# A state-space stage in fixed order on VectorE and GpSimd: states in fixed places, powers moved to VectorE, and two changed hand-overs of PSUM banks

## The chip, the cores and the metric

The kernel runs on one core of a Trainium2 chip. The core has a matrix engine (TensorE, PE in the profile), three engines for elementwise work (VectorE or DVE, ScalarE or ACT, GpSimd or POOL), and SyncE (SP), which here only issues loads. Each engine works through its own queue in order. The engines share an on-chip memory (SBUF) and wait for each other by semaphores; matrix products land in PSUM, which the kernel uses as eight banks of 128 x 512 float32. GpSimd does not touch PSUM in this kernel. The metric is the device time of one launch in microseconds, and smaller is better.

## The reference

One decoder layer on a sequence of 1024 tokens of width 1024, then a final RMS norm. From the normed and modulated input, one wide projection makes the inputs of two branches. Branch A gates in blocks of 128 tokens. Branch B is a causal convolution, then a chunked state-space scan:

```python
    decay = segsum_exp(adt)
    cb = jnp.einsum('bclgn,bcsgn->bcgls', cc, bc)
    y_diag = jnp.einsum('bcgls,bcgrls,bcsgrp->bclgrp', cb, decay, xd)
    chunk_states = jnp.einsum('bcsgn,bcgrs,bcsgrp->bcgrpn', bc, decay_to_end, xd)
    chunk_decay = jnp.exp(a_cs[..., -1])
    def step(state, inp):
        cs, cd = inp
        return state * cd[..., None, None] + cs, state
    _, prev_states = lax.scan(step, init, (chunk_states, chunk_decay))
    y_off = jnp.einsum('bclgn,bcgrpn,bcgrl->bclgrp', cc, prev_states, jnp.exp(a_cs))
    ...
    y_b = y_b + xh * d_skip[:, None]
    yz = (y_b * jax.nn.silu(ssm_z)).reshape(b, s, SSM_GROUPS, -1)
    y_b = rms_norm(yz, ssm_norm_w.reshape(SSM_GROUPS, -1))
    merged = jax.nn.sigmoid(g_a) * (y_a @ w_proj_a) + jax.nn.sigmoid(g_b) * (y_b @ w_proj_b)
    return x + gate[:, None, :] * (merged @ w_out)
```

There are 8 groups of 4 heads of 64 channels, 8 chunks of 128 tokens, and a state of 128 per channel. Everything is float32.

## The kernel before, in words

The kernel goes through stages that TensorE sets the pace of: the modulation and norm, a first block product (`v_block`), the other parts of the wide projection, the state-space stage together with branch A's output projection, branch B's output projection, the output product and the final norm. A float32 product is computed as three products of rounded parts (high x high, low x high, high x low; hence the `h` and `l` at the ends of names). The large block products are done in seven products per 2 x 2 blocks, named p1, p5, p6, p3, p7, p2, p4, each over some units k of 128 rows, into four PSUM banks j.

`v_block` (L815, its unit loop at L905 to L936) runs right after `sg`, the evacuations by ScalarE (L473) that free four PSUM banks which it then takes as `vx0` to `vx3`. Its first two units each go over the three terms and within each over the four banks; later units go bank by bank.

The state-space stage (class `Group`, L1040) works in 32 steps: groups in pairs, the two groups of a pair in turn, four steps of two chunks each. One step consists of:

- `fetch` (L1046): SP loads the five inputs `sl` and the decay exponents `dcy` into one of five buffers (`NSET = 5`), so a load waits until the step that used the buffer has read it for the last time, in the product yz on GpSimd (L1157).
- `decay` (L1062): ScalarE makes `ea` (L1067), GpSimd cuts off the upper triangle of `dcy` (the mask, an affine_select, L1070), ScalarE exponentiates (L1075).
- `prep` (L1077): TensorE makes `pc` and transposes into `pc` and `px` in PSUM. VectorE multiplies `px` into `xd` and `xe` (L1091) and `dcy` by `pc` (L1095); ScalarE copies the second half of `pc` to `bn` (L1097).
- `front` (L1100): TensorE computes `yi` (within a chunk) from `dcy` and `xd`, and `sp` (what a chunk adds to the state) from `xe` and `bn`. For each of the two chunks, GpSimd multiplies the state by the chunk's decay (L1123) and VectorE adds `sp` (L1125; the first state of a group is a copy, L1121). The state after the first chunk is called the middle state here, the one after the second the end state. New states go round through a ring of places `st_r`.
- `back` (L1129): TensorE computes `yn` from the state ahead of each chunk. `evacuate` (L1142): VectorE forms y1 = x * d_skip + yi (L1151, two instructions) and ym = yn * ea (L1155), GpSimd adds them (L1156) and multiplies by the gate into `yz` (L1157).
- `post` (L1159), every second step of a group: the result is stored to `yb_d`, and two tasks are put off: `squares` (L1174; two activations on ScalarE at L1176 in place, which wait until the store has read the data, and an addition on GpSimd at L1177) and `post2` (L1179; TensorE's sum `pq`, `ssq` on VectorE at L1186, and after a group's last part the power -1/2 of its eight norms on GpSimd at L1190). `later(n, f)` puts `f` off by n tasks; a step of the stage runs three (`front`, `back`, `prep`).

The PSUM banks of the stage are handed out in turn: `bank(name)` waits for the readers of the tile that had the bank eight hand-outs ago. So a TensorE instruction can wait for VectorE not because it needs a value but because it needs a bank: `yi` for the bank of an earlier `sp`, say.

Between the parts of a step TensorE is given instructions of branch A's output projection (`proj_a`, L1359; `draw(n)` takes the next n pieces). It accumulates `pma` over 8 k for each of 8 column blocks dd. At k = 1 `wa_block` (L1276) prepares the next block's weights: ScalarE rounds to `wah` (L1280), VectorE subtracts to get `wal` (L1281), each twice. At a block's end VectorE forms `tha` from `pma` (L1382) and stores it.

What sets the order: instructions wrapped in `pin` keep the order of the program; all others are placed on their engine's queue by a planner that goes by priorities (`tc.high_priority()`; `item` at L1410 gives it to every part of a step) and by its own idea of when operands are ready. In the kernel before, VectorE's and GpSimd's instructions of the state-space stage are of the second kind, and so is `wal`.

Branch B's output projection (`multiply`, L1545, matmul at L1552; unit loop from L1666) takes over the eight PSUM banks as `psx` and `psy` when p1 begins. `banks()` (L1443) hands them out in the order y0, y1, y2, x0 to x3, y3. The last `pma` tiles, the last `yn` and the last `pq` still hold some of them then.

The two hand-overs of banks that the diff touches are this order and the order of the first units of `v_block`.

## Time and profile before

| | us |
|---|---|
| median of 3 runs | 1404.81 (1404.6 to 1406.76) |
| profiled execution | 1402.83 |
| its span from first to last instruction | 1401.1 |
| mean clock granted to TensorE | 0.996 of full |

The profile's page gives the busy time of each engine, the span in 40 slices, the DMA queues, the chain of work that ended last, and the costliest groups. Other views give the busy time by windows, the waits of an engine by what ended them, and a timeline of one engine in order, in which the figure in brackets is the engine's idle time just before an instruction and what released it. The stages by time: `v_block` begins at 70.46 us, the state-space stage spans some 918 to 1145 us, and branch B's output projection (p1) begins at 1158.93 us.

| window, us | PE busy | DVE busy | ACT busy | POOL busy |
|---|---|---|---|---|
| 0 to 60 | 54.97 | 33.56 | 38.67 | 3.15 |
| 60 to 100 | 38.70 | 32.10 | 25.25 | 0.00 |
| 1140 to 1160 | 19.01 | 13.14 | 7.48 | 4.19 |
| 1260 to 1330 | 68.66 | 67.44 | 27.69 | 0.00 |

A window in which PE is busy all the time can't become shorter without less work for PE; where it is not, the timeline tells what it waited for.

### The profile page before, as it was taken

How to read it: one execution, taken by the hardware profiler on the slowest of the kernel's cores; microseconds unless marked ns; L12 is line 12 of the kernel's file. 1: busy time of each engine (PE TensorE's matmuls, PEld its weight loads, DVE VectorE, ACT ScalarE, POOL GpSimd, SP SyncE). 2: the span in 40 equal slices, each digit the busy share in tenths (PEclk: the TensorE clock that was granted, in tenths of full speed). 3: DMA queues.
4: the chain of work that ended last, by engine and by line, in shares of the span. 5: the costliest groups of instructions: out<-in, count | busy, mean ns of one | idle time of the engine just before them, and what ended most of it. 6: DMA issues, size and time to landing. Idle time of an engine off the chain costs nothing.

```text
span 1401.1 us, 20579 instructions
## 1 busy us (share of the span) xinstructions
PE 1369.7 (98%) x6971; PEld 1135.3 (81%) x6971; DVE 1055.3 (75%) x1815; ACT 804.7 (57%) x1496; POOL 217.8 (16%) x208
## 2 busy tenths in 40 slices
PE   8999999999999999999999999999999999999997
PEld 7678888888888888878888888888888788888786
DVE  4776776687777889888888795398777655859976
ACT  5754656666666566455675555677676623223453
POOL 0000000000000011211000110038878750000001
PEclk9999999999999999999999999999999999999999
DMA  8775433333434777777775774598887658878913
GB/s 263 197 237 147 120 121 120 105 123 118 135 105 128 225 219 230 220 238 226 215 220 148 241 214 134 179 354 319 279 267 278 220 185 280 319 254 313 378 44 120
DMA packets 277181, 288.62 MB, mean 206 GB/s; under 512 B 15788, under 2 KB 224084, under 8 KB 277076
## 3 DMA queue, kind: packets, MB, share of 16 engines
q1 hardware_dynamic: 182420, 203.76, 45.6%
q10 hardware_dynamic: 94656, 83.54, 18.1%
q8 instruction: 55, 0.90, 0.3%
q14 instruction: 50, 0.41, 0.1%
HBM read 199.79 MB, written 87.46 MB: 205 GB/s over the span
## 4 chain that ended last, share of the span: by engine, by line
PE 78%; DVE 7%; DMA 7%; ACT 3%; issue 3%; POOL 2%; SPq 1%; ACTq 0%; DVEq 0%; POOLq 0%
PE xuz L536 6%; PE xx L536 6%; PE xcb L536 6%; PE xz L536 5%; PE xg L536 5%; PE pma L81 4%; PE yx L536 3%; PE vx L918 3%; PE x L1552 3%; PE yuz L536 3%; PE yp L1552 3%; PE ycb L536 3%; PE yz L536 3%; PE ox L1745 2%; PE yg L536 2%
## 5 line engine op out<-in xcount | busy, mean ns | idle before, releaser
L759 POOL TENSOR_TENSOR wog<-wog,gb 128x256 f32<-128x256 f32 x16 | 21.5, 1362 | 624.0 <-DMA wog<-in_w_out_dram 602.9
L1075 ACT ACTIVATE dcy<-dcy,nacs 128x128 f32<-128x128 f32 x256 | 78.7, 388 | 17.2 <-POOL dcy L1070 16.1
L1070 POOL TENSOR_SCALAR_AFFINE_SELECT dcy<-dcy 128x1024 f32<-128x1024 f32 x32 | 35.0, 1094 | 135.4 <-DMA yl<-ya_d 88.7
L990 ACT ACTIVATE ac<-ac 128x1024 f32<-128x1024 f32 x32 | 33.9, 1060 | 25.8 <-DVE ac L988 22.6
L1067 ACT ACTIVATE ea<-dcy 64x512 f32<-64x512 f32 x64 | 40.0, 626 | 12.2 <-DMA dcy<-acs_d 11.8
L81 PE MATMUL pma<-yh,wah 128*128 128x512 f32 x128 | 43.8, 423 | 0.0
L81 PE MATMUL pma<-yh,wal 128*128 128x512 f32 x128 | 43.2, 419 | 0.0
L1490 DVE SCALAR_TENSOR_TENSOR yn<-yn,par,rb 128x512 f32<-128x512 f32 x32 | 23.9, 747 | 24.8 <-DMA yn<-yb_d 24.8
L1155 DVE TENSOR_TENSOR ym<-yn,ea 128x512 f32<-128x512 f32 (+1 forms) x32 | 19.9, 622 | 29.9 <-PE yn L81 29.7
L1095 DVE TENSOR_TENSOR dcy<-dcy,pc 128x1024 f32<-128x1024 f32 x32 | 38.9, 1217 | 3.8 <-PE pc L84 2.6
L1157 POOL TENSOR_TENSOR yz<-y,sl 128x512 f32<-128x512 f32 x32 | 41.4, 1294 | 1.1
L81 PE MATMUL pma<-yl,wah 128*128 128x512 f32 x128 | 40.3, 396 | 0.0
L1156 POOL TENSOR_TENSOR y<-y,ym 128x512 f32<-128x512 f32 (+1 forms) x32 | 36.6, 1143 | 14.5 <-DVE ym L1155 14.5
L81 PE MATMUL yi<-dcy,xd 128*64 128x128 f32 x512 | 35.9, 284 | 2.9 <-DVE st L1125 2.9
L81 PEld LDWEIGHTS yn<-sl,st 128*128 128x128 f32 x224 | 30.3, 190 | 8.8 <-issue 2.7
L81 PE MATMUL yn<-sl,st 128*128 128x128 f32 x224 | 31.4, 276 | 5.4 <-DVE st L1125 5.4
L81 PE MATMUL sp<-xe,bn 128*128 128x256 f32 x112 | 33.6, 418 | 2.9 <-DVE ssq L1186 1.7
L988 DVE SCALAR_TENSOR_TENSOR ac<-c2x,cwt,ac 128x1023 f32<-128x1023 f32 (+2 forms) x24 | 31.2, 1298 | 5.7 <-ACT ac L986 5.6
L1760 POOL TENSOR_TENSOR r<-r,fnw 128x512 f32<-128x512 f32 x2 | 2.5, 1296 | 208.2 <-ACT junk L1758 208.2
L988 DVE SCALAR_TENSOR_TENSOR ac<-c2cb,cwt,ac 128x1023 f32<-128x1023 f32 (+2 forms) x24 | 31.1, 1294 | 4.8 <-ACT ac L986 4.7
L1123 POOL TENSOR_TENSOR st<-st,cd 128x256 f32<-128x256 f32 x48 | 32.5, 677 | 11.2 <-PE yn L81 7.1
L952 ACT ACTIVATE vm<-vm,vr 128x128 f32<-128x128 f32 x64 | 25.8, 483 | 14.0 <-DMA vm<-v_d 13.5
...
## 6 DMA issues: line engine op xcount, KB each, us to landing
...
```

The costliest lines, as they stand in the source:

```text
L81: pin(PE.matmul(acc, l, r, start=first, stop=last))
L536: pin(PE.matmul(ps, lw[:, k * P : (k + 1) * P], r[k], start=first and n + k == 0, stop=n == 2 and k == 3, skip_group_check=not first))
L918: pin(PE.matmul(ps[pn][j], l[:, js], r, start=nm in ("p1", "p5", "p2") and n + k == 0, stop=n == 2 and k == 3, skip_group_check=nm not in ...
L988: V.scalar_tensor_tensor(ac[:, s:], cc[:, : S - s], conv_wt[:, 3 - s, i : i + 1], ac[:, s:], op0=ALU.mult, op1=ALU.add)
L990: A.activation(ac, ac, AF.Silu)
L1067: A.activation(ea[hh * HD : (hh + 1) * HD], dcy.rearrange("p (j e) i l -> p e j (i l)", e=2)[hh * HD : (hh + 1) * HD, hh], AF.Exp)
L1070: G.affine_select(out=d8, in_=d8, compare_op=ALU.is_ge, fill=-1e30, base=0, pattern=[[0, 2 * HPG], [1, P]], channel_multiplier=-1)
L1075: A.activation(dcy[:, h, i, :], dcy[:, h, i, :], AF.Exp, bias=sub[:, i, h : h + 1])
L1095: V.tensor_tensor(d3, d3, pc[:, 0:256].unsqueeze(1).to_broadcast([P, HPG, 256]), op=ALU.mult)
L1156: G.tensor_add(y1[:, :, t0:], y1[:, :, t0:], m[:, :, t0:])
L1157: G.tensor_mul(yz, y1, sl[:, 4:6])
L1552: pin(PE.matmul(ps[j], a[:, v, js], r, start=first and n + k == 0, stop=n == 2 and k == KT - 1, skip_group_check=not first))
```

## The change

In `v_block`, the first two units' matmuls are drawn together: first the eight high x high and low x high products of both units on banks 0 and 1, then the rest. In the state-space stage VectorE's and GpSimd's instructions are pinned to the order of the program (those of `prep` not in the first pair's first step). The order in `prep` becomes `dcy` times `pc`, then `bn` (now copied by VectorE), then `xd`, `xe`. States live in six fixed places, three for each group of a pair: one for the middle state and two in turn for the end state. `front` now adds the middle state, issues GpSimd's multiplication for the end state, and forms y1, which was in `evacuate`. A new `close`, called after `back`, adds `sp` to the end state (so behind ym on VectorE) and issues GpSimd's multiplication for the next step's middle state. `squares` is put off by 8 tasks instead of 5. The power -1/2 is made by 11 small VectorE instructions (128 x 8) instead of one on GpSimd: a first guess from the exponent bits, then three rounds of three. The subtraction `wal` is pinned at k = 3 and k = 4 of `proj_a`. At the start of p1, PSUM banks are handed out in the order y0, y2, x0 to x3, y3, y1.

VectorE's instructions become 120 more (32 copies and 8 x 11 small ones), ScalarE's 32 fewer and GpSimd's 8 fewer.

```diff
                 ps["y"] = [bank(f"vy{j}") for j in range(4)]
-            (bh, bl), (wh, wl) = (bop[bn][v][k] for v in range(2)), wops[u]
-            terms = list(enumerate(((bh, wh), (bl, wh), (bh, wl))))
-            for j, (n, (l, r)) in [(j, t) for t in terms for j in range(4)] if u < 2 else [(j, t) for j in range(4) for t in terms]:
-                js = slice(j * P, (j + 1) * P)
-                pin(PE.matmul(ps[pn][j], l[:, js], r, start=nm in ("p1", "p5", "p2") and n + k == 0,
+            at = [(u, n, j) for j in range(4) for n in range(3)]
+            if u == 0:
+                ends = [(0, 2, 0), (0, 2, 1)] + [(0, n, j) for j in (2, 3) for n in range(3)]
+                at = [(i, n, j) for i in range(2) for n in range(2) for j in range(2)] + ends
+            elif u == 1:
+                at = [(1, 2, 0), (1, 2, 1)] + [(1, n, j) for j in (2, 3) for n in range(3)]
+            for i, n, j in at:
+                (bh, bl), (wh, wl) = (bop[bn][v][units[i][1]] for v in range(2)), wops[i]
+                l, r = ((bh, wh), (bl, wh), (bh, wl))[n]
+                pin(PE.matmul(ps[pn][j], l[:, j * P : (j + 1) * P], r, start=nm in ("p1", "p5", "p2") and n + units[i][1] == 0,
                               stop=n == 2 and k == 3, skip_group_check=nm not in ("p1", "p5", "p2")))
-            wops.pop(u)
+            if u:
+                wops.pop(u)
...
     NSET = 5
-    nstep, nst = [0], [0]
+    nstep = [0]
...
                 tp(px[:, i * 256 + P : i * 256 + 256], sl[:, 3, tsl], ident)
+            keep = pin if s or g > 1 else lambda i: i
             x4 = px.rearrange("p (i h w) -> p i h w", i=2, h=HPG)
             xs = []
+            d3 = dcy.rearrange("p h i l -> p h (i l)")
+            keep(V.tensor_tensor(d3, d3, pc[:, 0:256].unsqueeze(1).to_broadcast([P, HPG, 256]), op=ALU.mult))
+            bn = p2x.tile([P, 256], F32, name=f"bn{nm}", tag="bn", bufs=2)
+            keep(V.tensor_copy(bn, pc[:, 256:512]))
             for v, f in (("xd", dthq), ("xe", dde)):
                 t = p2x.tile([P, 512], F32, name=f"{v}{nm}", tag=v, bufs=3)
-                V.tensor_tensor(t.rearrange("p (i h w) -> p i h w", i=2, h=HPG), x4,
-                                fac(f, g, s).unsqueeze(3).to_broadcast([P, 2, HPG, HD]), op=ALU.mult)
+                keep(V.tensor_tensor(t.rearrange("p (i h w) -> p i h w", i=2, h=HPG), x4,
+                                     fac(f, g, s).unsqueeze(3).to_broadcast([P, 2, HPG, HD]), op=ALU.mult))
                 xs.append(t)
-            d3 = dcy.rearrange("p h i l -> p h (i l)")
-            V.tensor_tensor(d3, d3, pc[:, 0:256].unsqueeze(1).to_broadcast([P, HPG, 256]), op=ALU.mult)
-            bn = p2x.tile([P, 256], F32, name=f"bn{nm}", tag="bn", bufs=3)
-            A.copy(bn, pc[:, 256:512])
             self.pre[s] = (sl, dcy, bn, xs[0], xs[1], ea)
...
             sp = bank(f"sp{nm}")
-            self.y[s] = yi
-            self.sts = [self.st]
-            for i in range(2 if s < NCH // 2 - 1 else 1):
+            last = s == NCH // 2 - 1
+            for i in range(1 if last else 2):
                 mm(sp[:, i * 256 : (i + 1) * 256], bn[:, i * P : (i + 1) * P], xe[:, i * 256 : (i + 1) * 256])
-            for i in range(2 if s < NCH // 2 - 1 else 1):
-                pool, tag, b = st_r[nst[0] % 4 if nst[0] % 4 < 3 else 2]
-                nst[0] += 1
-                s2 = pool.tile([P, 512 if pool is hp else 256], F32, name=f"st{nm}_{i}", tag=tag, bufs=b)[:, 0:256]
-                if self.st is None:
-                    V.tensor_copy(s2, sp[:, 0:256])
-                else:
-                    G.tensor_mul(v3(s2), v3(self.st),
-                                 fac(cd, g, s)[:, i].unsqueeze(2).to_broadcast([P, HPG, HD]))
-                    V.tensor_add(s2, s2, sp[:, i * 256 : (i + 1) * 256])
-                self.st = s2
-                self.sts.append(s2)
+            mid, *ends = state(g % 2)
+            if s == 0:
+                pin(V.tensor_copy(mid, sp[:, 0:256]))
+            else:
+                pin(V.tensor_add(mid, mid, sp[:, 0:256]))
+            self.sts = [self.st, mid]
+            self.st = ends[s % 2]
+            if not last:
+                pin(G.tensor_mul(v3(self.st), v3(mid), fac(cd, g, s)[:, 1].unsqueeze(2).to_broadcast([P, HPG, HD])))
+            self.y1 = y1 = turn(y1_r, f"y1{nm}", F32).rearrange("p (j t) -> p j t", j=2)
+            for j in range(2):
+                pin(V.scalar_tensor_tensor(y1[:, j], sl[:, 2 + j], dskt[:, 2 * g + j : 2 * g + j + 1],
+                                           yi[:, j * 256 : (j + 1) * 256], op0=ALU.mult, op1=ALU.add))
+            self.sp = sp
+
+        def close(self, s):
+
+            if s == NCH // 2 - 1:
+                return
+            v3 = lambda t: t.rearrange("p (h w) -> p h w", h=HPG)
+            mid = state(self.g % 2)[0]
+            pin(V.tensor_add(self.st, self.st, self.sp[:, 256:512]))
+            pin(G.tensor_mul(v3(mid), v3(self.st), fac(cd, self.g, s + 1)[:, 0].unsqueeze(2).to_broadcast([P, HPG, HD])))
...
                            sl[:, 0, i * P : (i + 1) * P])
-            self.evacuate(s, self.y.pop(s), yn)
+            self.evacuate(s, self.y1, yn)
             if s % 2:
...
-        def evacuate(self, s, yi, yn):
+        def evacuate(self, s, y1, yn):
...
             yz = self.yz[s // 2][:, :, (s % 2) * 256 : (s % 2 + 1) * 256]
-            y1 = turn(y1_r, f"y1{nm}", F32).rearrange("p (j t) -> p j t", j=2)
-            for j in range(2):
-                V.scalar_tensor_tensor(y1[:, j], sl[:, 2 + j], dskt[:, 2 * g + j : 2 * g + j + 1],
-                                       yi[:, j * 256 : (j + 1) * 256], op0=ALU.mult, op1=ALU.add)
             m = turn(ym_r, f"ym{nm}", F32).rearrange("p (j t) -> p j t", j=2)
             t0 = 0 if s else P
-            V.tensor_tensor(m[:, :, t0:], yn.rearrange("p (j l) -> p j l", j=2)[:, :, t0:], ea[:, :, t0:], op=ALU.mult)
-            G.tensor_add(y1[:, :, t0:], y1[:, :, t0:], m[:, :, t0:])
-            G.tensor_mul(yz, y1, sl[:, 4:6])
+            pin(V.tensor_tensor(m[:, :, t0:], yn.rearrange("p (j l) -> p j l", j=2)[:, :, t0:], ea[:, :, t0:], op=ALU.mult))
+            pin(G.tensor_add(y1[:, :, t0:], y1[:, :, t0:], m[:, :, t0:]))
+            pin(G.tensor_mul(yz, y1, sl[:, 4:6]))
...
             if g < NG - 2 or q == 0:
-                later(5, self.squares, yz, [yz[:, j] for j in range(2)])
+                later(8, self.squares, yz, [yz[:, j] for j in range(2)])
                 later(17, self.post2, q, [yz[:, 0]])
...
                     mm(pq[:, i : i + 1], t[:, i * P : (i + 1) * P], ones[:, 0:1], j == 0, j == len(sq) - 1)
-            with tc.high_priority():
-                V.tensor_scalar(ssq[:, g * NCH + q * 4 : g * NCH + q * 4 + 4], pq[:, 0:4], 1.0 / 256, EPS,
-                                op0=ALU.mult, op1=ALU.add)
+            pin(V.tensor_scalar(ssq[:, g * NCH + q * 4 : g * NCH + q * 4 + 4], pq[:, 0:4], 1.0 / 256, EPS,
+                                op0=ALU.mult, op1=ALU.add))
             if q == 1:
-                c8 = slice(g * NCH, (g + 1) * NCH)
-                G.tensor_tensor(ssq[:, c8], ssq[:, c8], nhalf, op=ALU.pow)
+                t, v = (ssq[:, n % NG * NCH : (n % NG + 1) * NCH] for n in (g, g + 2))
+                pin(V.tensor_scalar(sc.bitcast(I32), t.bitcast(I32), -0.5, float(0x5F3759DF), op0=ALU.mult, op1=ALU.add))
+                pin(V.tensor_scalar_mul(v, t, -0.5))
+                for n in range(3):
+                    pin(V.tensor_mul(t, sc, sc))
+                    pin(V.tensor_mul(t, t, v))
+                    pin(V.scalar_tensor_tensor(t if n == 2 else sc, t, 1.5, sc, op0=ALU.add, op1=ALU.mult))
                 if g < NG - 2:
...
-    war_r, wah_r, wal_r = [], [], []
+    war_r, wah_r, wal_r, lows = [], [], [], []
...
             A.copy(wh, wr)
-            V.tensor_sub(wl, wr, f32(wh))
+            if dd == 0:
+                V.tensor_sub(wl, wr, f32(wh))
+            else:
+                lows.append((wl, wr, wh))
             was[dd].append((wh, wl))
...
                     wa_block(dd + 1)
+                elif k in (3, 4) and lows:
+                    wl, wr, wh = lows.pop(0)
+                    pin(V.tensor_sub(wl, wr, f32(wh)))
             keep = pin if dd == KT - 1 else lambda i: i
...
     tha_r, ea_r, y1_r, ym_r = (ring(c) for c in (4, 3, 2, 2))
-    st_r = [(hp, room.pop(0), 1), (p2x, "st", 1), (p2q, "st", 2)]
+    st_tag = room.pop(0)
+    st2 = hp.tile([P, 512], F32, name="st2", tag=st_tag)
+    sts = [st2[:, 0:256], st2[:, 256:512]]
+    sts += [pool.tile([P, 256], F32, name=f"st{n}", tag="st", bufs=2) for pool in (p2x, p2q) for n in range(2)]
+
+    def state(n):
+        return sts[n], sts[2 + n], sts[4 + n]
+
     fetch(4)
...
         step(n, "back")
+        with tc.high_priority():
+            groups[order[n][0]].close(order[n][1])
         if n == 1:
...
-    room.extend(ea_r[0] + [st_r[0][1]])
+    room.extend(ea_r[0] + [st_tag])
     room.extend(tag for k in range(KT - 2) for tag in ya_tags[k])
...
             if nm == "p1":
-                psy = banks("yp3", "y", 3)
-                psx = banks("x", "x")
-                psy += [psb.tile([P, 512], F32, name="yp33", tag="by3")]
+                first = {t: psb.tile([P, 512], F32, name=f"{t}p", tag=f"b{t}") for t in ('y0', 'y2', 'x0', 'x1', 'x2', 'x3', 'y3', 'y1')}
+                psx, psy = ([first[f"{v}{j}"] for j in range(4)] for v in "xy")
                 rows_bank[0] = lambda name: psy[("pq6_1", "pq7_1", "pr6", "pr7").index(name)]
...
                 psy = banks(f"y{nm}", "y")
```

4 lines of the change are left out of this document (2 added, 2 removed).

## The prediction

> **What bounds the kernel now.** I read the page first, then the window table over the state-space stage, then TensorE's gaps one by one in the timeline, then what stood on the other engines just ahead of each gap. TensorE carries the kernel:
>
> ```profile
> PE 1369.7 (98%) x6971; PEld 1135.3 (81%) x6971; DVE 1055.3 (75%) x1815; ACT 804.7 (57%) x1496; POOL 217.8 (16%) x208
> ```
>
> 31 us of the span are not PE-busy. The window table shows where the stage of the change loses some (columns: window, length, then busy us of PE, PEld, DVE, ACT and POOL with counts, the granted clock, DMA share, GB/s):
>
> ```profile
> 930.00:960.00 30.00, 29.95 (x215) 25.66 (x215) 23.95 (x44) 21.17 (x58) 20.20 (x22) 1.00 0.94 313
> 990.00:1020.00 30.00, 29.15 (x234) 25.55 (x232) 20.35 (x38) 20.87 (x57) 25.83 (x25) 1.00 0.75 261
> 1020.00:1050.00 30.00, 27.52 (x208) 23.88 (x206) 23.26 (x45) 20.98 (x54) 21.40 (x22) 1.00 0.82 271
> 1050.00:1080.00 30.00, 28.09 (x219) 24.71 (x221) 22.43 (x42) 20.82 (x57) 26.69 (x26) 1.00 0.77 267
> 1080.00:1110.00 30.00, 26.56 (x185) 23.01 (x186) 18.11 (x35) 20.78 (x53) 19.32 (x20) 0.89 0.73 253
> 1110.00:1140.00 30.00, 28.09 (x225) 24.42 (x224) 20.74 (x39) 9.66 (x25) 22.43 (x22) 1.00 0.43 149
> ```
>
> In the first window PE loses 0.05 us, so the stage can run full; from 1020 on each window loses 2 to 3.4. DVE and POOL are near 80% there, so neither is the bound, but both are close enough that the order of their queues matters. The gaps on PE that the changed parts can touch (start, duration, instruction, in brackets the gap and what ended it):
>
> ```profile
> 72.61 0.50 PE L918 MATMUL vx<-p1v0h,b11h 128*128 128x512 f32 x1 [1.30 <-ACT sg L473]
> 979.80 1.10 PE L81 MATMUL sp<-xe,bn 128*128 128x256 f32 x4 [0.63 <-DVE xe L1091]
> 1002.61 0.57 PE L81 MATMUL yn<-sl,st 128*128 128x128 f32 x3 [0.85 <-DVE st L1125]
> 1024.35 0.68 PE L81 MATMUL yn<-sl,st 128*128 128x128 f32 x4 [2.14 <-DVE st L1125]
> 1050.23 0.68 PE L81 MATMUL yn<-sl,st 128*128 128x128 f32 x4 [0.57 <-DVE st L1125]
> 1078.08 0.68 PE L81 MATMUL yn<-sl,st 128*128 128x128 f32 x4 [1.68 <-DVE st L1125]
> 1094.65 0.67 PE L81 MATMUL sp<-xe,bn 128*128 128x256 f32 x2 [0.57 <-DVE xe L1091]
> 1102.45 1.97 PE L81 MATMUL yi<-dcy,xd 128*64 128x128 f32 x16 [2.87 <-DVE st L1125]
> 1127.95 1.10 PE L81 MATMUL sp<-xe,bn 128*128 128x256 f32 x4 [1.71 <-DVE ssq L1186]
> 1158.93 0.50 PE L1552 MATMUL x<-p1bh,p1a 128*128 128x512 f32 x1 [0.99 <-DVE tha L1382]
> ```
>
> They sum to 13.3 us. Behind the 2.87 the granted clock falls: 0.89 over 30 us is 3.3 us of clock, an estimate of the loss that this gap drags along. 13.3 + 3.3 = 16.6 us is the most that the change can gain here. What held VectorE at these gaps, in the timelines and groups (a group row: count, then busy us and mean ns, then idle time and its releasers):
>
> ```profile
> 1019.73 0.70 DVE L1281 TENSOR_TENSOR wal<-wa,wah 128x512 fp32r<-128x512 f32 x1 [1.83 <-ACT wah L1280]
> L1281 DVE TENSOR_TENSOR wal<-wa,wah 128x512 fp32r<-128x512 f32 x14 | 10.8, 778 | 5.0 <-ACT wah L1280 4.9
> 1045.89 0.42 DVE L1125 TENSOR_TENSOR st<-st,sp 128x256 f32<-128x256 f32 x1 [3.92 <-POOL st L1123]
> L1176 ACT ACTIVATE yz<-yz 128x512 f32<-128x512 f32 x28 | 17.5, 628 | 16.5 <-DMA yb_d<-yz 16.2
> 1098.93 1.27 ACT L1067 ACTIVATE ea<-dcy 64x512 f32<-64x512 f32 x2 [2.46 <-DMA dcy<-acs_d]
> 1100.26 1.09 POOL L1070 TENSOR_SCALAR_AFFINE_SELECT dcy<-dcy 128x1024 f32<-128x1024 f32 x1 [4.20 <-ACT ea L1067]
> 1101.32 0.61 POOL L1123 TENSOR_TENSOR st<-st,cd 128x256 f32<-128x256 f32 x1
> 1101.97 0.42 DVE L1125 TENSOR_TENSOR st<-st,sp 128x256 f32<-128x256 f32 x1 [5.76 <-POOL st L1123]
> ```
>
> So there are three kinds. At 1002, 1024 and 1078 VectorE's queue had the subtraction wal in front of a state addition, and wal waited for ScalarE's cast wah. At 1050 and 1128 it waited for the state multiplication on GpSimd, which stood behind other work there; ScalarE's squares L1176, which wait 16.2 us in all for the store of yb_d, hold up what GpSimd waits for. At 1102 a load of dcy came late, ScalarE and the mask on GpSimd with it, and the state multiplication was queued behind the mask.
>
> **The change part by part.**
>
> Bank transitions. In v_block the fourth matmul waited 1.30 for the fourth bank, the one that sg frees last. Now ten on the first two banks and three on the third come ahead of it: ten more cover the 1.30 even if each took but a third of the 0.50 shown (they overlap). At p1 the last evacuation (tha) now holds a bank that is written last, not first. Gain 1.30 + 0.99 = 2.29, bounds 0 (operands late instead) and 2.6 (the first gap also fills and drains the pipe).
>
> The subtraction wal. It is pinned two and three k-steps behind the cast, so it can't wait for it: 0.85 + 2.14 + 1.68 = 4.67 gained. Its own 0.7 us stays, now between y1 and ym. Behind ym stand the end addition and the next dcy; what is late next is ym by at most 0.7, covered as below. Bounds 3 to 4.7.
>
> Squares at 8 instead of 5: three tasks, one step, some 7 us later (32 steps in the 227 us from 918 to 1145). A wait for yb_d is 16.2 / 28 = 0.6 on the mean, so the 16.2 us on ScalarE go, with the two activations and GpSimd's addition moved behind the store. No DMA moves with it. With the states' fixed order on GpSimd this takes 0.57 + 1.71 = 2.28; bounds 0 and 2.3.
>
> The gap of 2.87 with its clock. In the new order the mask of the next dcy still stands ahead of that state multiplication on GpSimd, the end addition still frees the PSUM bank that yi needs, and the load is still paced by SP, which waits for GpSimd's product yz:
>
> ```profile
> SPq L90 <- POOL yz L1157: 104.7, 27, 8.6
> ```
>
> yz keeps its place in the step, so the load isn't issued much earlier. I take 0; bounds 0 and 2.87 + 3.3 = 6.2.
>
> What it costs. These rows price the copy bn, now on VectorE (nearest: its state copy from PSUM, same shape), the power that leaves GpSimd, and one step on VectorE in which a power falls, with the slack behind it, and the ym of another such step; the last two are a chain of eight dependent small operations at the kernel's end, first and next after last:
>
> ```profile
> L1097 ACT COPY bn<-pc 128x256 f32<-128x256 f32 x32 | 11.7, 367 | 21.7 <-DVE dcy L1095 21.3
> L1121 DVE COPY st<-sp 128x256 f32<-128x256 f32 x8 | 3.3, 416 | 0.9 <-PE sp L81 0.9
> L1190 POOL TENSOR_TENSOR ssq<-ssq,nhalf 128x8 f32<-128x8 f32 x6 | 9.9, 1646 | 0.0
> L1155 DVE TENSOR_TENSOR ym<-yn,ea 128x512 f32<-128x512 f32 (+1 forms) x32 | 19.9, 622 | 29.9 <-PE yn L81 29.7
> 1007.55 0.15 DVE L1186 TENSOR_SCALAR ssq<-pq 128x4 f32<-128x4 f32 x1
> 1007.62 0.86 DVE L1151 SCALAR_TENSOR_TENSOR y<-sl,dskt,yi 128x256 f32<-128x256 f32 x2
> 1008.40 0.41 DVE L1125 TENSOR_TENSOR st<-st,sp 128x256 f32<-128x256 f32 x1
> 1010.05 0.69 DVE L1155 TENSOR_TENSOR ym<-yn,ea 128x512 f32<-128x512 f32 x1 [1.24 <-PE yn L81]
> 1064.03 0.69 DVE L1155 TENSOR_TENSOR ym<-yn,ea 128x512 f32<-128x512 f32 x1 [2.18 <-PE yn L81]
> 1395.34 0.14 DVE L1730 TENSOR_SCALAR dde<-dde 128x1 int32<-128x1 int32 x1
> 1396.99 0.48 DVE L1844 TENSOR_SCALAR r<-r,dde 128x512 f32<-128x512 f32 x1
> ```
>
> bn: about 0.35 us a step (0.416 less the overlap of neighbours). VectorE waits 29.7 us in 32 steps for yn, 0.93 a step, and y1 (0.78 from 1007.62 to 1008.40) moves behind the state addition, so the addition that yn needs comes 0.78 - 0.35 = 0.43 earlier than now. Only where PE already waits for xe (0.63 and 0.57) does bn lengthen the gap: 2 x 0.35 = 0.7. Bounds 0 and 0.35 x 32 less the slack, still 0.7. ScalarE loses the copy and 21 us of waiting.
>
> Power. Eight operations take 1396.99 - 1395.34 = 1.65, 0.206 each; eleven take 2.27, eight times, two of them in p1 where VectorE has room. In the step shown, ssq would end at 1007.62 + 0.35, the power at 1010.24, the middle state at 1010.6; yn's second half, four matmuls that take about 0.6 (0.68 in the gap rows), now starts near 1010.05 - 0.6 = 1009.45: 1.15 late. Where ym waits 2.18 and not 1.24, 0.94 more is covered and 0.2 is left; I put the other five at 0.15 each: 1.9 in all. The nearest row for contention says more:
>
> ```profile
> 1049.68 1.09 POOL L1070 TENSOR_SCALAR_AFFINE_SELECT dcy<-dcy 128x1024 f32<-128x1024 f32 x1
> 1050.03 1.28 DVE L1281 TENSOR_TENSOR wal<-wa,wah 128x512 fp32r<-128x512 f32 x1
> ```
>
> wal took 1.28 instead of 0.70: it ended 0.54 after the mask did, as if it had begun only then. Nine of the eleven operations read two SBUF operands like wal. If the first of each power waits out half of a GpSimd operation of 1.09, with GpSimd busy 0.86 of the time (25.83 of 30), that is 6 x 0.47 = 2.8 more: 4.7. I take 3.5, between the two, since GpSimd often has run dry by then (it waits for the middle state). Bounds 0 and 6 x 2.27 = 13.6.
>
> The new fixed order otherwise: end addition ahead of the next dcy, multiplications pinned. GpSimd is busy 26.69 of 30 us at most, and the 9.9 us of powers leave it. I take 0; its bad end is the rival on the other side.
>
> Sum: 2.29 + 4.67 + 2.28 = 9.24 gained, 0.7 + 3.5 = 4.2 lost, net 5.0. The profiled execution took 1402.83 (span 1401.1 and 1.73 around it), so 1397.8; the median of the runs, 1404.81, stands 2.0 above it, so 1399.8 on that footing. I forecast 1398.5, between.
>
> **The rivals.** The late load. Without bn's 21 us on ScalarE and the powers on GpSimd, masks come earlier, yz and with it SP's loads too; if the gap at 1102 closes with its clock, 6.2 more: about 1392, and 1390 with a power at 1.9. For it: the mask waited 4.20, and 2.46 of it is the load. Against: the load itself took the time, on DMA engines at 0.73 to 0.94.
>
> The lock. If not one but two GpSimd operations pass between the small ones of each power, 6 x 2 x 1.09 = 13 us of waiting, of which the slack and the longer steps take some 4: the power costs 1.9 + 9 and nothing remains of the gain: 1402 to 1407. For it: the 1.28 above. Against: the row is one of 512 columns, and a power reads 8. The Trainium skill's SBUF — State Buffer, Who interferes with whom, states it as a rule: a VectorE instruction with two SBUF inputs and a GpSimd instruction that reads SBUF exclude each other, and the later one blocks fully. By that rule these eleven operations are the wrong ones for VectorE in this stage; the 1.28 agrees with it.
>
> Slower: the end addition. VectorE now can't begin the next dcy before GpSimd has multiplied the end state, and masks are queued ahead of that:
>
> ```profile
> L1070 POOL TENSOR_SCALAR_AFFINE_SELECT dcy<-dcy 128x1024 f32<-128x1024 f32 x30 | 32.8, 1094 | 43.0 <-ACT ea L1067 43.0
> ```
>
> A mask waits 1.4 us on the mean. It decides once the wait exceeds a step's slack of 0.93: 0.5 x 30 = 15 us lost, less the 5.0 gained: 1404.81 + 10 = about 1415, and half of that 1410. Against: the multiplication is due a whole yn earlier than the addition.
>
> **How the numbers follow.** No change that a measurement can tell is 0.2%, 2.8 us: 1402.0 to 1407.6. Forecast (1394 to 1402): 0.49. Late load gone (1388 to 1394): 0.20. Lock (1402 to 1407): 0.14. Slower (1408 to 1415): 0.17. Hence faster 0.69, same 0.14, slower 0.17. The range 1389 to 1409 leaves out some 0.05 below and 0.13 above; the likeliest case alone spans 1394 to 1402.
>
> **What would show it.** Right: no gap on PE released by sg near 72 or tha near 1158; no wal that waits for wah; no squares that wait for yb_d; gaps of yn only at the six steps with eleven small operations, below 1.2 us each. The lock: small operations of 0.5 us and more beside a GpSimd operation. Slower: state additions on VectorE released by GpSimd in most steps, and PE gaps at pc, yi or sp behind them. The forecast is wrong if the gap behind the late load grows or closes, as the clock makes each such gap count twice.

## The result: slower by 0.8%

The changed kernel takes 1418.27 us (median of 5, 1415.56 to 1419.84) against 1406.18 for the kernel before (median of 5, 1404.6 to 1410.73). The ratio is 1.0082 with a 95% interval of 1.0062 to 1.0102. The forecast was 1398.5 and its range ended at 1409, so sign and range both missed. The profiled execution took 1415.56 us (span 1413.5), 12.7 above the one before. One execution of e14 below, which took 2967.8 us, is left out of its figures.

In the profile's first table, TensorE (PE) is still the engine that is nearly always busy, with the same 6971 matmuls, but is listed as busy for 7.8 us more. The work is the same; the mean clock granted to it fell from 0.996 to 0.989.

```profile
PE 1377.5 (97%) x6971; PEld 1141.6 (81%) x6971; DVE 1089.1 (77%) x1935; ACT 795.5 (56%) x1464; POOL 209.4 (15%) x200
```

The window table of the changed kernel (window, length, busy us of PE, PEld, DVE, ACT and POOL, granted clock, DMA share, GB/s) shows the first hand-over of banks repaired and four windows of the state-space stage below full clock. The other 30 us windows of the stage are at 1.00.

```profile
60.00:100.00 40.00, 40.00 (x193) 30.75 (x192) 32.44 (x55) 25.00 (x46) 0.00 (x0) 1.00 0.70 227
930.00:960.00 30.00, 27.00 (x180) 23.02 (x179) 23.61 (x42) 17.35 (x46) 18.96 (x20) 0.94 0.75 252
1020.00:1050.00 30.00, 27.46 (x195) 24.17 (x196) 24.67 (x52) 17.20 (x44) 20.28 (x19) 0.89 0.71 235
1050.00:1080.00 30.00, 27.26 (x193) 24.11 (x192) 26.13 (x52) 20.01 (x51) 23.17 (x24) 0.89 0.76 270
1080.00:1110.00 30.00, 26.84 (x201) 23.31 (x200) 22.84 (x51) 18.61 (x48) 17.84 (x18) 0.95 0.75 249
```

The same view with one window over the whole stage, from the first matmul into `pma` to the first of p1, for the kernel before (p1 begins there at 1156.42; the matmul at 1158.93, named above as its start, is the first of p1 that waits):

```profile
918.79:1156.42 237.63, 226.35 (x1654) 195.62 (x1652) 173.32 (x316) 152.24 (x390) 167.11 (x162) 0.99 0.78 268
```

and for the changed kernel:

```profile
916.02:1165.97 249.95, 232.91 (x1653) 201.15 (x1652) 203.71 (x411) 141.88 (x356) 158.67 (x156) 0.96 0.74 254
```

So the stage alone became 12.3 us longer. Of that, 5.8 are time in which PE isn't busy (17.0 against 11.3; the single gaps of the timeline add to 16.8 and 11.2) and 6.6 are PE busy for longer with the same work. The clock columns give nearly the same second figure: 0.06 x 30 + 0.11 x 30 twice + 0.05 x 30 = 9.9 us lost, against 3.3 before. So the added gaps came with about as much again in clock. Behind the start of p1 2.8 us more were lost, and the stage begins 2.8 earlier, 1.3 of which is the gap in `v_block`.

What PE waited for in the stage of the changed kernel, from the view of waits (waiting line and what released it: us in total, times, longest):

```profile
PE yn L81 <- DVE st L1126: 9.4, 5, 3.5
PE sp L81 <- DVE ssq L1198: 4.0, 3, 1.7
PE px L84 <- DVE tha L1405: 2.7, 1, 2.7
PE yi L81 <- issue: 0.5, 1, 0.5
PE yn L81 <- DVE y L1133: 0.3, 1, 0.3
```

Before, the gaps of yn were 5.4 us in five, those of sp 2.9 in three, and the one of yi was 2.87. So yn costs 4.0 more, sp 1.1 more, px is new with 2.7, and the gap of yi is gone. The largest, from PE's timeline of the changed kernel (start, duration, instruction, gap and releaser in brackets), with two behind p1's start:

```profile
936.35 0.69 PE L84 MATMUL px<-ident,sl 128*128 128x128 f32 x2 [2.72 <-DVE tha L1405]
...
1022.54 1.20 PE L81 MATMUL yn<-sl,st 128*128 128x128 f32 x4 [3.55 <-DVE st L1126]
...
1071.90 0.68 PE L81 MATMUL yn<-sl,st 128*128 128x128 f32 x4 [2.74 <-DVE st L1126]
...
1107.18 2.05 PE L81 MATMUL sp<-xe,bn 128*128 128x256 f32 x4 [1.67 <-DVE ssq L1198]
...
1184.40 0.27 PE L84 MATMUL y2p<-ident,ssq 128*8 128x128 f32 x1 [1.63 <-DVE ssq L1207]
...
1188.80 0.27 PE L84 MATMUL y3p<-ident,ssq 128*8 128x128 f32 x1 [1.37 <-DVE ssq L1207]
```

### The profile page after: what moved, and what is told of

Read it like the earlier page. It is cut to its first block, busy times and chain, and to the rows that moved or that the text cites. A ratio compares the mean times of both kernels' runs of the same rounds, so it can differ in the third digit from the quotient of the medians.

```text
span 1413.5 us, 20656 instructions
## 1 busy us (share of the span) xinstructions
PE 1377.5 (97%) x6971; PEld 1141.6 (81%) x6971; DVE 1089.1 (77%) x1935; ACT 795.5 (56%) x1464; POOL 209.4 (15%) x200
## 3 DMA queue, kind: packets, MB, share of 16 engines
q10 hardware_dynamic: 94656, 83.54, 17.9%
## 4 chain that ended last, share of the span: by engine, by line
PE 69%; DMA 13%; DVE 9%; issue 3%; ACT 2%; POOL 2%; SPq 1%; ACTq 1%; DVEq 0%; POOLq 0%
PE xuz L536 6%; PE xx L536 5%; PE xcb L536 5%; PE xz L536 5%; PE xg L536 3%; PE yuz L536 3%; PE vx L923 3%; PE yx L536 3%; PE ycb L536 3%; PE ox L1776 2%; PE pma L81 2%; PE yz L536 2%; PE oy L1776 2%; DMA yb_d<-yz 2%; PE acc L81 2%
## 5 line engine op out<-in xcount | busy, mean ns | idle before, releaser
L1169 POOL TENSOR_TENSOR y<-y,ym 128x512 f32<-128x512 f32 (+1 forms) x32 | 36.5, 1141 | 25.7 <-DVE ym L1168 25.7
L1168 DVE TENSOR_TENSOR ym<-yn,ea 128x512 f32<-128x512 f32 (+1 forms) x32 | 19.9, 622 | 16.7 <-PE yn L81 16.2
L994 DVE SCALAR_TENSOR_TENSOR ac<-c1cb,cwt,ac 128x1023 f32<-128x1023 f32 (+2 forms) x24 | 31.6, 1318 | 1.3 <-ACT ac L992 1.3
```

The lines of the kernel that those rows point to most:

```text
L994: V.scalar_tensor_tensor(ac[:, s:], cc[:, : S - s], conv_wt[:, 3 - s, i : i + 1], ac[:, s:], op0=ALU.mult, op1=ALU.add)
L1169: pin(G.tensor_add(y1[:, :, t0:], y1[:, :, t0:], m[:, :, t0:]))
```

## The experiments

Executions of one kernel spread over several us, with the clock that each was granted: the kernel before lies between 1398 and 1414 in its runs beside the experiments, and the part from the first matmul of `v_block` to the stage, the same in nearly all kernels, lasts 846 to 855 us in the profiles. So medians of all executions are shown (n of them), and beside them the parts of the one profiled execution: the stage, the sum of PE's gaps in it, and the time from the start of p1 to the end. The sums of gaps repeat only roughly: kernels whose stages have the same program differ in them by about 1 us (16.8 and 17.9; 15.4, 14.2 and 14.9; 11.5 and 12.5).

| kernel | median us (n) | ratio to before (95%) | stage | gaps in it | p1 to end |
|---|---|---|---|---|---|
| before | 1406.2 (5) | | 237.6 | 11.2 | 244.7 |
| after | 1418.3 (5) | 1.0082 (1.0062 to 1.0102) | 250.0 | 16.8 | 247.5 |
| e1_after_pow | 1413.0 (10) | 1.0053 (1.0029 to 1.0077) | 239.8 | 11.5 | 248.5 |
| e4_before_power | 1416.0 (4) | 1.0080 (1.0048 to 1.0111) | 242.8 | 13.8 | 245.7 |
| e2_after_psum | 1418.4 (5) | 1.0078 (1.0053 to 1.0103) | 241.6 | 15.4 | 251.0 |
| e10_psum_p1 | 1415.7 (11) | 1.0074 (1.0052 to 1.0096) | 243.0 | 14.2 | 248.6 |
| e11_after_p1 | 1416.9 (7) | 1.0082 (1.0054 to 1.0111) | 250.1 | 17.9 | 244.7 |
| e13_psum_stage | 1419.8 (5) | 1.0099 (1.0069 to 1.0129) | 241.3 | 14.9 | 247.4 |
| e14_pow_stage | 1412.4 (10) | 1.0051 (1.0035 to 1.0067) | 242.1 | 12.5 | 245.8 |
| e3_before_banks | 1403.2 (10) | 0.9973 (0.9957 to 0.9990) | 237.4 | 11.5 | 243.1 |
| e7_before_banks_wal | 1407.6 (10) | 1.0009 (0.9991 to 1.0026) | 240.8 | 12.4 | 242.2 |
| e5_after_post2 | 1409.0 (10) | 1.0006 (0.9987 to 1.0025) | 239.3 | 13.0 | 248.0 |
| e6_after_post2_ym | 1407.6 (10) | 1.0006 (0.9982 to 1.0030) | 235.5 | 8.8 | 247.9 |
| e9_ym_p1 | 1406.1 (11) | 0.9995 (0.9973 to 1.0018) | 236.3 | 11.0 | 244.2 |
| e12_ym_p1_wal | 1409.9 (11) | 1.0022 (0.9998 to 1.0046) | 236.1 | 10.3 | 246.3 |
| e8_after_order_act | 1427.5 (4) | 1.0155 (1.0108 to 1.0203) | 258.8 | 24.4 | 244.3 |

### The power on VectorE

First, the power alone is put back on GpSimd in the changed kernel (e1), and alone put on VectorE in the kernel before (e4, with priority and no pin).

```diff
 # e1, from the changed kernel
-                t, v = (ssq[:, n % NG * NCH : (n % NG + 1) * NCH] for n in (g, g + 2))
-                pin(V.tensor_scalar(...)) ... and the ten behind it
+                c8 = slice(g * NCH, (g + 1) * NCH)
+                G.tensor_tensor(ssq[:, c8], ssq[:, c8], nhalf, op=ALU.pow)
 # e4, from the kernel before: the same lines the other way, under tc.high_priority()
```

> The changed kernel with one part undone: the power -1/2 is one operation on GpSimd again, everything else stays. Theory P (the eleven operations on VectorE, lengthened by GpSimd, are the main loss): the five waits of yn for a state addition (9.4 us), the two waits of p1's transposes for the power (3.0) and most of the lowered clock of 1020 to 1080 (6.6) go; 1418.3 - 17 = about 1401, 1397 to 1405. Theory O (the fixed order itself is the loss): 1412 or more, with the yn gaps still there.

> The kernel before with the power on VectorE alone (eleven operations at high priority, no pin). Theory P: it alone costs most of the 12 us: 1413 to 1420. If the planner, which may put other work between the operations, hides it: 1406 to 1409; then it is the power in a fixed order that costs, not the power.

Measured: 5.3 us less on the median in the changed kernel, and 9.5 more in the kernel before. The stage fell from 250.0 to 239.8 and rose from 237.6 to 242.8. The gaps of yn behind a state addition fell from 9.4 to 1.2 us, as the first theory of e1 said, but the time is in the range of the second (1412 or more). The power is the largest single part of the loss that was measured, and it is less than half of the 12.1 us. The two medians of 5.3 us difference are uncertain by some 3.

VectorE's timeline in one step of the changed kernel shows how a power of 2.27 us by the prediction's count takes 5.01 from its first row to the state addition (1016.98 to 1021.99):

```profile
1016.98 0.15 DVE L1198 TENSOR_SCALAR ssq<-pq 128x4 f32<-128x4 f32 x1
1017.17 0.80 DVE L1202 TENSOR_SCALAR sc<-ssq 128x8 int32<-128x8 int32 x1
1017.88 0.16 DVE L1203 TENSOR_SCALAR ssq<-ssq 128x8 f32<-128x8 f32 x1
1018.07 1.24 DVE L1205 TENSOR_TENSOR ssq<-sc 128x8 f32<-128x8 f32 x1
1019.35 0.53 DVE L1206 TENSOR_TENSOR ssq<-ssq 128x8 f32<-128x8 f32 x1
...
1021.12 0.94 DVE L1207 SCALAR_TENSOR_TENSOR ssq<-ssq,sc 128x8 f32<-128x8 f32 x1
1021.99 0.41 DVE L1126 TENSOR_TENSOR st<-st,sp 128x256 f32<-128x256 f32 x1
```

GpSimd's timeline beside it:

```profile
1016.65 1.29 POOL L1169 TENSOR_TENSOR y<-y,ym 128x512 f32<-128x512 f32 x1
1018.01 1.28 POOL L1170 TENSOR_TENSOR yz<-y,sl 128x512 f32<-128x512 f32 x1
1019.25 0.61 POOL L1144 TENSOR_TENSOR st<-st,cd 128x256 f32<-128x256 f32 x1
1020.91 1.13 POOL L1076 TENSOR_SCALAR_AFFINE_SELECT dcy<-dcy 128x1024 f32<-128x1024 f32 x1 [1.05 <-ACT ea L1073]
```

The four long operations end at 1017.97, 1019.31, 1019.88 and 1022.06; GpSimd's operations end at 1017.94, 1019.29, 1019.86 and 1022.04. It is the same in all six powers of the stage: every operation with two SBUF inputs that began 0.05 us or more after a GpSimd operation still running (eight of them) ended 0.02 to 0.03 us after it. L1198, whose input is in PSUM, took 0.15 beside a running GpSimd operation. This is what the Trainium skill states in SBUF — State Buffer, Who interferes with whom; the trace agrees for operations with two SBUF inputs of eight columns. L1202, an int32 operation with a single SBUF tensor as input, waited too, in all six powers; the same section says that a tensor_scalar can take the shared ports in some of its modes, but no run here shows in which mode this one ran.

This step is one of the worst. The six powers of the stage take 2.56, 5.01, 4.37, 6.65, 2.19 and 4.62 us from their first row to the state addition; inside the 6.65 stands a `tha` that waited 1.89 for its load. The waits of the small operations, which is what they take beyond 0.17 each, sum to 9.4 us over the six; the prediction had put 2.8 for them, and its lock rival 13.

If the wait is the lock, it must go when one input of each operation is in PSUM. e2 puts the scaled value and the products there; e10 is e2 and e11 the changed kernel, both with the transposes of the last two groups' norms one unit later in p1, which was meant to remove the two gaps there; e13 and e14 are e11 with the PSUM form, or GpSimd's power, for the six groups in the stage alone.

```diff
 # e2, from the changed kernel (e13: for g < NG - 2 alone)
-                t, v = (ssq[:, n % NG * NCH : (n % NG + 1) * NCH] for n in (g, g + 2))
+                t = ssq[:, g * NCH : (g + 1) * NCH]
+                v, w = (pq[:, 8 * n : 8 * n + 8] for n in (1, 2))
...
-                    pin(V.tensor_mul(t, sc, sc))
-                    pin(V.tensor_mul(t, t, v))
-                    pin(V.scalar_tensor_tensor(t if n == 2 else sc, t, 1.5, sc, op0=ALU.add, op1=ALU.mult))
+                    pin(V.tensor_mul(w, sc, v))
+                    pin(V.tensor_mul(w, w, sc))
+                    pin(V.scalar_tensor_tensor(t if n == 2 else sc, w, 1.5, sc, op0=ALU.add, op1=ALU.mult))
 # e10, e11, e13, e14: beside that
-        if nm == "p1" and k in (3, 4):
-            groups[NG - 5 + k].post3()
+        if nm == "p1" and k in (4, 5):
+            groups[NG - 6 + k].post3()
```

> The changed kernel with the same eleven operations in the same places, but two of the four operands in PSUM, so that nine of ten operations behind the first read at most one SBUF operand. Theory P with the lock (a VectorE operation with two SBUF operands waits for GpSimd): no small operation but the first is longer than 0.25 us, each power takes 2.3 to 3 us from its ssq to the state addition (now 2.2 to 5.0, and 6.6 with a tha inside), the time falls by some 6 to 10: 1408 to 1412. Rival (the length of eleven dependent operations alone): operations stay long or the time stays at 1416 to 1420.

> The changed kernel with the power's operands in PSUM and the transposes one k later, to be held against the next run, which differs from it only in where the power's operands are. If waiting for GpSimd is most of the power's price: state-space stage of 241 to 243 us (250 in the changed kernel), time 6 to 9 us below the next run: about 1407. If the length of eleven dependent operations is the price: within 3 us of the next run.

> The changed kernel with the transposes of p1 one k later, nothing else. Theory: the gaps of 1.6 and 1.4 us in p1 go, the stage stays at 250 us: 1418.3 - 3 = 1415. Rival: 1418.

> The changed kernel with the transposes one k later, and the six powers of the state-space stage with operands in PSUM; the two of p1 as in the changed kernel (in the run with all eight in PSUM, p1 had a new gap of 4.89 us that hid the effect). Held against the run with the transposes alone later (1416.9). If the waiting of the small operations for GpSimd is most of the price: stage of 241 to 243 us, part behind p1 as there (244 to 246), time 1408 to 1411. If it isn't: 1414 to 1418.

> The same, with the six powers of the stage on GpSimd, the two of p1 on VectorE as in the changed kernel. It gives the whole price of the six powers: stage of 239 to 240 us, time 1406 to 1408; the difference to the run with PSUM operands is the price of eleven dependent operations that wait for nobody, 1 to 4 us. Theory O (the fixed order is the loss): 1412 or more.

The groups by line (count, then busy us and mean ns, then idle time before them) of the changed kernel:

```profile
L1205 DVE TENSOR_TENSOR ssq<-sc 128x8 f32<-128x8 f32 x18 | 6.1, 341 | 0.6
L1206 DVE TENSOR_TENSOR ssq<-ssq 128x8 f32<-128x8 f32 x18 | 4.6, 257 | 0.6
L1202 DVE TENSOR_SCALAR sc<-ssq 128x8 int32<-128x8 int32 x6 | 3.8, 639 | 0.2
```

and of e2:

```profile
L1206 DVE TENSOR_TENSOR pq<-sc,pq 128x8 f32<-128x8 f32 x18 | 3.1, 171 | 0.6
L1207 DVE TENSOR_TENSOR pq<-pq,sc 128x8 f32<-128x8 f32 x18 | 3.1, 174 | 0.6
L1203 DVE TENSOR_SCALAR sc<-ssq 128x8 int32<-128x8 int32 x6 | 3.2, 530 | 0.2
```

With one input in PSUM an operation takes 171 to 174 ns on the mean instead of 257 to 341, while the int32 operation, whose input stayed in SBUF, still waits. In the stage of e2, 24 of the 54 operations with an input in PSUM ran beside a GpSimd operation for 0.1 us or more, and none of the 54 took more than 0.18. So the lock is shown at the operation. The stage by one window of e11, e13 and e14, in three fences:

```profile
919.00:1169.09 250.09, 232.05 (x1653) 200.08 (x1652) 204.38 (x412) 141.71 (x356) 158.61 (x156) 0.97 0.73 253
```

```profile
921.26:1162.51 241.25, 226.14 (x1654) 194.79 (x1652) 196.22 (x411) 141.40 (x356) 158.01 (x156) 0.99 0.76 262
```

```profile
919.33:1161.43 242.10, 229.59 (x1653) 197.99 (x1651) 182.38 (x345) 140.74 (x356) 166.70 (x162) 0.97 0.76 261
```

In gaps, the power in the stage costs 17.9 - 12.5 = 5.4 us (e11 against e14). The lock is some 3 of it (e13: 14.9), and what is left, 14.9 - 12.5 = 2.4, is the length of the eleven operations. With the spread between kernels of the same stage these are 4.3 to 6.4, 1.4 to 3.7 and 1.7 to 3.9. In medians the power in the stage costs 4.5 us (1416.9 against 1412.4), but the PSUM forms gained nothing that is certain: 1418.4 against 1418.3, 1415.7 and 1419.8 against 1416.9.

The profiled stages of these kernels are 7 to 9 us shorter, so e10 and e13 met what was expected of their stages (241 to 243) and missed their times (about 1407, and 1408 to 1411), as e2 missed its 1408 to 1412. The record shows two reasons. The first is the luck of the profiled execution: of the 8.8 us by which the stage of e13 is shorter than that of e11, 5.9 are PE busy for less time with the same work, since the clock was halved in one stretch of 3.41 us there and in five in e11 (last section). That execution was the fastest of e13 (1411.67, at a mean clock of 0.996, its other four 1418.4 to 1421.2 at 0.991 to 0.993), and the profiled one of e2 its fastest too. The second is p1, where part of it is lost again: 2.7 us in e13 and 3.9 in e10, both against e11, and 3.5 in e2 against the changed kernel. The later transposes left 0.28 us of gaps at their place in e11, but a gap of 4.89 stands in p1 in e10, and one of 3.70 in e13. How much of the whole time is the lock's stays open. e14 missed its forecast too: 1406 to 1408 was expected, and 1412.4 is in the range of its rival, that the fixed order is the loss.

### The hand-overs of banks

Only the two hand-overs are put into the kernel before.

```diff
 # e3, from the kernel before: the new order of v_block's first two units, and in p1
-                psy = banks("yp3", "y", 3)
-                psx = banks("x", "x")
-                psy += [psb.tile([P, 512], F32, name="yp33", tag="by3")]
+                first = {t: psb.tile([P, 512], F32, name=f"{t}p", tag=f"b{t}") for t in ('y0', 'y2', 'x0', 'x1', 'x2', 'x3', 'y3', 'y1')}
+                psx, psy = ([first[f"{v}{j}"] for j in range(4)] for v in "xy")
```

> The kernel before with the two hand-overs of PSUM banks alone (order of v_block's first two units; order of p1's banks). If local gains reach the end: 1406.2 - 1.30 - 0.99 = 1403.9 (1402.5 to 1405). If they are given back later: 1406 (within 0.1%).

Measured: 1403.24, 3.2 us less than the kernel before beside it (1406.48), ratio 0.9973 (0.9957 to 0.9990). This is the best kernel of the study and beats both.

### The subtraction wal

e7 is e3 with `wal` put off and pinned as in the change. e12 is e9 (below) with `wal` as it was before.

```diff
 # e7, from e3 (e12: the same lines the other way, from e9)
-            V.tensor_sub(wl, wr, f32(wh))
+            if dd == 0:
+                V.tensor_sub(wl, wr, f32(wh))
+            else:
+                lows.append((wl, wr, wh))
...
+                elif k in (3, 4) and lows:
+                    wl, wr, wh = lows.pop(0)
+                    pin(V.tensor_sub(wl, wr, f32(wh)))
```

> The kernel before with the two hand-overs of banks and with wal put off to k = 3 and 4, nothing else. My forecast's term: the three waits of yn behind wal (0.85 + 2.14 + 1.68) go, 4.7 us less than with the banks alone (1403.2): 1398.5. Rival: in the planner's order something else is late at these steps: 1402 to 1404.

> As the first run of these, but with wal where the planner puts it, as before the change. My forecast's term: three waits of yn behind wal come back, 4.7 us more: about 1408.5. Rival (putting wal off gains nothing, as it cost 4 us in the order before): the same or less than the first run, 1401 to 1404.

In the order before (e7 against e3), the stage got 3.4 us longer, not 4.7 shorter, and the median rose by 4.4. Of the 3.4, 0.9 are in the gaps; the rest is PE busy for longer with the same work. The waits of VectorE show what became of the gain. In e3:

```profile
DVE wal L1287 <- ACT wah L1286: 8.4, 6, 2.4
DVE st L1131 <- POOL st L1129: 14.0, 9, 3.1
```

In e7, where `wal` has no such row among the large waits:

```profile
DVE st L1131 <- POOL st L1129: 20.1, 15, 2.9
```

So 6.1 of the 8.4 us came back as waits for GpSimd's state multiplication. These are sums over the whole execution; that each of them stands right behind a moved `wal` is argued, not shown.

In the changed order (e12 against e9) the answer is open. With `wal` back in the planner's place VectorE waits for `wah` 10.5 us in four times instead of 2.9 in one, yet the stage (236.1 and 236.3) and its gaps (10.3 and 11.0) are the same in the profiles. The median of e12 is 3.8 us above that of e9, 1409.9 against 1406.1, close to the 1408.5 that the forecast's term would give; the ratios' intervals overlap a little. So the profiles speak against the term there, and the medians for it.

### The fixed order and the first units of p1

e5 is e1 with `ssq` (L1198) free under priority, not pinned. e6 is e5 with `ym` of the first pair's first step free too. e9 is e6 with the transposes one unit later in p1.

```diff
 # e5, from e1
-            pin(V.tensor_scalar(ssq[...], pq[:, 0:4], 1.0 / 256, EPS, op0=ALU.mult, op1=ALU.add))
+            with tc.high_priority():
+                V.tensor_scalar(ssq[...], pq[:, 0:4], 1.0 / 256, EPS, op0=ALU.mult, op1=ALU.add)
 # e6, from e5, in evacuate
+            keep = pin if s or g > 1 else lambda i: i
-            pin(V.tensor_tensor(m[:, :, t0:], ...
+            keep(V.tensor_tensor(m[:, :, t0:], ...
```

> The changed kernel with ssq and the power as before (ssq at high priority and not pinned, power on GpSimd). In the run with the power alone undone, two transposes of p1 still waited 0.74 and 3.37 us for the power, whose ssq stood pinned on VectorE behind a yn that waited for its load. Theory (the pin of ssq): these two gaps go and the part behind p1's start is 243 to 245 us long again (248.5 with the pin); the whole is 4 us shorter than that run, about 1409. Rival (the order of banks or something else in p1): the gaps stay, 1413.

> As the run before it, and ym and what follows it are not pinned in the first step of the first pair, so that ym needn't stand behind a tha that waits for its load (2.7 us on TensorE near 936 us in the changed kernel, and a clock of 0.94 behind it). Theory: the gap on px near 936 goes, with its clock: 3 to 4 us less than the run before it, about 1405. Rival: the load is late anyhow and another instruction waits: no difference.

> As the run with ssq and power as before and ym free, and the two transposes of the last two rows in p1 come one k later. In that run they still waited 0.65 and 3.39 us for the power, whose ssq stands on VectorE behind a yn that waits for its load (the pin was not the reason). Theory: both gaps go, the part behind p1's start is 243 to 245 us (247.9 without), the whole 3 to 4 us less than 1407.6: about 1404. Rival: the rows are then late for the next stage: no gain.

The gap of px at 936.35 has its origin here, in VectorE's timeline of the changed kernel:

```profile
930.06 1.29 DVE L1402 TENSOR_TENSOR wal<-wa,wah 128x512 fp32r<-128x512 f32 x2 [2.86 <-ACT wah L1297]
...
934.89 1.41 DVE L1405 SCALAR_TENSOR_TENSOR tha<-tha,pma 128x512 f32<-128x512 f32 x2 [2.42 <-DMA tha<-th_d]
936.21 0.42 DVE L1168 TENSOR_TENSOR ym<-yn,ea 128x256 f32<-128x256 f32 x1
```

The first `tha` isn't pinned, and the planner put it ahead of the pinned `ym`; its load was late by 2.42 us, and `ym`, the state addition and PE's px stood behind it. With `ym` free (e6) it went ahead of `tha`, px waited 0.51 instead of 2.49 (e5), a new gap of 1.52 at the next yn came, and the stage fell by 3.9 us in the profile; the median fell by 1.4, within what the intervals allow for nothing.

For p1 I held the pin of `ssq` responsible. That fell: the gaps of p1 are 4.1 us in e1 and 4.1 in e5. VectorE's timeline of e1 shows the cause:

```profile
1172.45 0.75 DVE L1517 SCALAR_TENSOR_TENSOR yn<-yn,par,rb 128x512 f32<-128x512 f32 x1 [3.49 <-DMA yn<-yb_d]
...
1173.72 0.15 DVE L1198 TENSOR_SCALAR ssq<-y0p 128x4 f32<-128x4 f32 x1
```

`ssq` stands behind a product that waited 3.49 us for a load of yb_d, pinned or not. With the transposes one unit later PE waits less there: p1 to the end took 244.2 in e9 against 247.9 in e6, with a gap of 1.94 left, and 244.7 in e11 against 247.5 in the changed kernel.

Why e5 beats e1 by 4.0 us on the median, with separate intervals, while stage and p1 of their profiles differ by 0.9, isn't explained.

### The squares

In the stage, ScalarE's squares waited for their store longer than before, not less. The view of waits, for the kernel before:

```profile
ACT yz L1176 <- DMA yb_d<-yz: 16.2, 12, 2.6
```

for the changed kernel:

```profile
ACT yz L1189 <- DMA yb_d<-yz: 25.7, 17, 3.4
```

and for e8 (e6 with the squares, their addition, the mask and the exponentials of `decay` pinned as well; in e6 itself the wait is 17.4 us in 14 times):

```profile
ACT yz L1191 <- DMA yb_d<-yz: 8.2, 3, 3.7
```

```diff
 # e8, from e6
-                A.activation(sq[j], yz[:, j], AF.Square)
-            G.tensor_add(sq[0], sq[0], sq[1])
+                pin(A.activation(sq[j], yz[:, j], AF.Square))
+            pin(G.tensor_add(sq[0], sq[0], sq[1]))
 # and keep(...) around the two exponentials and the affine_select of decay
```

> As the run with ym free, and ScalarE's squares and exponentials and GpSimd's masks and sums of squares pinned too, so that the squares really come later than the store of yb_d. In the changed kernel ScalarE waits 25.7 us for that store (16.2 before), although the squares are put off by 8 tasks instead of 5. Theory: that wait falls below 10 us and the gaps of sp for ssq go: 3 to 5 us less than the run with ym free, about 1401. Rival: exponentials and masks, now behind the squares, come late for yi: longer than the run with ym free.

So the number 8 didn't reach ScalarE's queue: the squares aren't pinned, and the planner places them where it thinks them ready. Once they are pinned (e8), half of their wait goes, 17.4 to 8.2, and the stage becomes 23 us longer than in e6 (PE waits 7.2 us for states, 6.7 for xe, 3.6 for ScalarE's exponentials). So these pins together cost far more than the waits did; which of them does, squares, masks or exponentials, was not told apart. That holding back the squares alone would gain nothing isn't shown.

## Why the prediction failed, step by step

The step that failed is the sum of the state-space stage, on both of its sides: gains were booked for waits that go (4.67 for `wal`, 2.28 for the squares), and the new fixed order was put at 0. e9 shows the size of this apart from the power. There the power is on GpSimd, and `ssq`, the first `ym` and the transposes of p1 are mended. Without its power term the forecast's sum gives 1406.2 - 9.24 + 0.7 = 1397.7 for such a kernel; it took 1406.1. So 8.4 us less was gained than the sum has, although the hand-overs of banks, 2.29 in the sum, gain 3.2 by themselves. On top of this came the power, 4.5 to 5.3 us by medians in place of 3.5.

- **Bank transitions: right.** Forecast 2.29; the window from 60 us is now full (38.70 busy before, 40.00 now), no gap ends at `tha` near p1 in the changed kernel, and e3 measured 3.2 (interval 1.4 to 6.0). In e3 0.76 of the second gap remained, at a later product.
- **The subtraction wal.** "It can't wait for it: 4.67 gained" has two parts. The first is wrong once: `wal` waited 2.86 us for `wah` at 930.06. The second is refuted in the order before, where taking the waits away gained nothing and VectorE went on to wait for GpSimd's states (e7). In the changed order it stays open (e12). Its 0.7 us was asked after; what VectorE would wait for next was not.
- **Squares: the step "the 16.2 us on ScalarE go" failed.** They became 25.7, so no run shows the 2.28 as gained. The step took a count of tasks for a place in the queue; `squares` isn't pinned, and its place was the planner's.
- **The gap of 2.87 with its clock.** Taken as 0. That gap went, but 1.67 came in its neighbourhood, with the clock halved behind it (last section). The prediction named the growing or closing of this gap as a sign that it is wrong.
- **bn: right at one of its two places.** The gap in front of sp at 982.05 is 0.96 instead of 0.63, as forecast (0.35). The second place can't be told apart in the changed order. The slack that was to cover the rest did shrink:

```profile
DVE ym L1168 <- PE yn L81: 16.2, 17, 2.1
```

  against 29.7 us before; bn and the longer powers share it.
- **Power: mechanism right, mis-sized.** Forecast 3.5 of loss. In gaps it is 5.4 in the stage, and in the medians 4.5 (e14) to 5.3 (e1, with p1), beside 9.5 alone in the kernel before. The waits of the small operations sum to 9.4 instead of 2.8. The single gaps reach 3.55 and 2.74 where 0.2 to 1.2 were worked out. "GpSimd often has run dry by then" holds for two of the six powers (2.56 and 2.19 us); in the step shown the power met four GpSimd operations, not half of one. "Two of them in p1 where VectorE has room" was wrong too: PE waited 1.63 and 1.37 there.
- **The new fixed order otherwise: taken as 0.** It cost the gap of px (2.72). In p1 the transposes, which the change left in place, met late loads. The ladder of medians tells the sizes, each step uncertain by 2 to 3 us: 1418.3 (after), 1413.0 with the power on GpSimd (e1), 1409.0 with `ssq` free (e5), 1407.6 with `ym` free (e6), 1406.1 with later transposes (e9), 1403.2 with nothing but the bank hand-overs (e3). By these medians the rest of the change, even without the power and mended, gives away what the bank hand-overs gain. How that divides among states, `bn`, squares and `wal` was not told apart.
- **The clock.** The text said that the clock makes each gap count twice, yet no cost in its sum carried that factor. 6.6 of the stage's 12.3 us are PE busy for longer at a lower clock: six stretches of half clock, 10.2 us, where the kernel before has two, 3.4. This is one execution of each.
- **Rivals.** The lock was seen at work as the rival described it, but the time came out above its 1402 to 1407, and it wasn't alone. The slower rival forecast about 1415, near what came, but its mechanism shows at two gaps only: ahead of those of sp at 1107.18 (1.67) and 1136.15 (1.37) end additions waited 0.89 and 0.32 us for GpSimd. In all, VectorE's end additions wait for GpSimd 2.7 us in the changed kernel,

```profile
DVE st L1143 <- POOL st L1130: 2.7, 5, 1.0
```

  where the state additions of the kernel before waited:

```profile
DVE st L1125 <- POOL st L1123: 13.7, 8, 5.8
```

  The second row holds middle and end additions together; the middle additions of the changed kernel have no such row. So the fixed order did shorten this wait, while PE's gaps of yn behind state additions grew from 5.4 to 9.4.
